# Feed-forward tokens normalised in halves, and the down projection's right factors made in the up phase

## The chip, the cores and the metric

The kernel runs on one core of a Trainium2 chip. The core has five engines that work side by side: TensorE (PE in the profile; its weight loads are PEld), VectorE (DVE), ScalarE (ACT), GpSimd (POOL) and SyncE (SP), which here only issues DMAs. Each engine takes its instructions strictly in the order in which the program was scheduled, and they wait for one another with semaphores. The metric is the device time of one execution in microseconds; lower is better.

## What is computed

One inference step of a two-layer decoder over 1024 prompt tokens, 16 learned tokens in front of them, and 8 x 8 sample tokens: 1104 token columns in layer 0 and 1088 in layer 1. The width is 1024 (`KD` = 8 blocks of 128 rows), the feed-forward width `D_FF` is 2816 (22 blocks of 128).

```python
def _trunk(h, ...):
    for layer in range(DEPTH):                        # 2
        if layer < N_A_LAYERS:                        # layer 0: Mamba-2
            mix, c, s = _mamba2_mixer(_rmsnorm(h, ssm_norm_g), ...)
        else:                                         # layer 1: window attention
            kv_in = _rmsnorm(h, kv_norm_g)            # shared K and V
            hn = _rmsnorm(h, attn_norm_g)
            mix = _sliding_sink_attention(hn @ w_q, k_all, v_all, ...) @ w_o
        h = h + mix
        hn = _rmsnorm(h, ffn_norm_g[layer])
        h = h + (jax.nn.silu(hn @ ffn_w_gate[layer]) * (hn @ ffn_w_up[layer])) @ ffn_w_down[layer]
    y = _rmsnorm(h, final_norm_g)
```

## The kernel before

**Arithmetic.** The data are float32. Every factor of a product is split into a high part H (a cast, on ACT) and a low part L (source minus H, a subtraction), and one product is three matmuls: H·H, H·L, L·H (`mm`, L1290 to L1293). The feed-forward products use a Strassen-Winograd scheme with seven products instead of eight (`PRODUCTS`): the left factors are the weight blocks A11 to A22 and four sums S1 to S4 of them, the right factors are the activation blocks B11 to B22 and the differences T1, T2, T3 and N4. Each product belongs to one of three PSUM lanes; the results are gathered from the lanes.

**Up phase** (`up`). The normalised tokens are cut into two row halves and two column halves, `h` = 552 columns each (544 in layer 1), so B11 and B21 belong to one half of the tokens, B12 and B22 to the other. A unit j is one block of 128 gate columns and one of 128 up columns; there are 22. A unit is seven products of 24 matmuls, 3696 matmuls per layer. `factor` (L1115 to L1123) makes one weight factor: ACT casts H (L1121), POOL subtracts L (L1122), and the sums S1 to S4 are made by DVE (L1113). After each product, `after_up` gathers lanes and applies the gate on DVE and ACT (L1327 to L1345) and sends the finished activations to DRAM (`act`).

**In front of the up phase** stands `normalise`. It starts when every residual column is done: sums of squares in `tot` (POOL, L1017), `row_scale` (L1028 to L1034 and the reciprocal root), `col_scale` (L1048 diagonals, a matmul L1049, a copy L1050), then for all 1104 columns the scaling (L1311), the differences (L1186) and the splits of seven right factors (ACT L1319, L by DVE or POOL L1320). The first steps of `up` are products 1 and 2 of two units, and wait for these splits.

**Down phase** (`down`). Five chunks of two Strassen units (1680 matmuls, tile `dacc`), then the last two row blocks as plain products (144 wide matmuls in layer 0, the same work by parts in layer 1; tile `wacc`, L69 to L71). The activations come back from DRAM (`ar`); DVE makes their differences (`bt`, L1186), ACT and DVE split them (`bo`, L1383 and L1384), POOL makes the weight sums and their low parts. The results are added to the residual tiles `hN` (DVE L1434; the sums X, Y, Z of the last chunk by POOL, L1437). In layer 0 the shared key and value product (`rps`) follows; at the end of layer 1 the final norm follows (transposes L1524, `Y` L1527, scaling L1542 and L1544).

**Order.** A tile scheduler turns this program into one list for each engine. SP's list holds all loads and stores, in one order.

## Time and profile before

| what | us |
|---|---|
| median of 3 runs | 3146.96 |
| lowest and highest run | 3145.66 and 3148.99 |
| the profiled execution's own time | 3141.77 |
| its span | 3140.0 |
| granted TensorE clock, mean | 0.958 |

The profile is one execution. Its span, from the first to the last instruction, is shorter than the execution's own time by 1.8 us. Busy shares of an engine over the span mix stages with different limits, so the stages are read apart: Mamba to about 1058, the first up phase to 1584, the first down phase to 1866, projections and attention to 2213, the output projection w_o to 2317, the second up phase to 2842, the second down phase with the final norm to 3140.

### The profile page before, as it was taken

How to read it: one execution, taken by the hardware profiler on the slowest of the kernel's cores; microseconds unless marked ns; L12 is line 12 of the kernel's file. 1: busy time of each engine (PE TensorE's matmuls, PEld its weight loads, DVE VectorE, ACT ScalarE, POOL GpSimd, SP SyncE). 2: the span in 40 equal slices, each digit the busy share in tenths (PEclk: the TensorE clock that was granted, in tenths of full speed). 3: DMA queues.
4: the chain of work that ended last, by engine and by line, in shares of the span. 5: the costliest groups of instructions: out<-in, count | busy, mean ns of one | idle time of the engine just before them, and what ended most of it. 6: DMA issues, size and time to landing. Idle time of an engine off the chain costs nothing.

```text
span 3140.0 us, 50718 instructions
## 1 busy us (share of the span) xinstructions
PE 2879.9 (92%) x19756; PEld 2607.1 (83%) x19756; DVE 2007.2 (64%) x3205; ACT 1132.2 (36%) x2296; POOL 1641.7 (52%) x1476
## 2 busy tenths in 40 slices
PE   7888989997999589999989989999967999998997
PEld 7777988875777489999989977766757999998997
DVE  6789676578685655545489970255246545548996
ACT  3444443344433332222233342356323222223332
POOL 2677565368564354444477763322225444447775
PEclk9999999998999789999999999999988999999999
DMA  4433423243332132222252120111013222225211
GB/s 117 130 119 103 143 85 108 90 136 114 98 111 77 58 118 77 74 78 77 82 179 86 41 69 21 43 35 31 14 57 110 73 79 76 83 73 186 83 43 65
DMA packets 298731, 270.17 MB, mean 86 GB/s; under 512 B 18604, under 2 KB 257644, under 8 KB 297950
## 3 DMA queue, kind: packets, MB, share of 16 engines
q1 hardware_dynamic: 298490, 266.92, 27.3%
q8 instruction: 156, 2.56, 0.3%
q14 instruction: 85, 0.69, 0.1%
HBM read 216.48 MB, written 50.40 MB: 85 GB/s over the span
## 4 chain that ended last, share of the span: by engine, by line
PE 65%; DVE 13%; POOL 4%; issue 3%; ACT 1%; DMA 0%; SPq 0%; POOLq 0%; ACTq 0%; DVEq 0%
PE wacc L1293 10%; PE wacc L1291 10%; PE wacc L1292 10%; PE acc L69 3%; PE acc L70 3%; PE acc L71 3%; PE dacc L1291 3%; PE dacc L1293 3%; PE dacc L1292 3%; DVE bt L1186 2%; DVE bo L1384 2%; PE rps L71 1%; PE rps L69 1%; PE rps L70 1%; PE ps L1734 1%
## 5 line engine op out<-in xcount | busy, mean ns | idle before, releaser
L1122 POOL TENSOR_TENSOR wo<-sum,wo 128x512 fp32r<-128x512 f32 x256 | 354.8, 1387 | 356.5 <-PE wacc L1293 247.2
L1122 POOL TENSOR_TENSOR wo<-ws,wo 128x512 fp32r<-128x512 f32 x216 | 300.4, 1394 | 331.0 <-PE wacc L1293 189.3
L1291 PE MATMUL dacc<-bo,wo 128*128 128x276 f32 (+1 forms) x1120 | 332.7, 300 | 29.3 <-DVE hN L1434 9.0
L1292 PE MATMUL dacc<-bo,wo 128*128 128x276 f32 (+1 forms) x1120 | 327.5, 293 | 6.6 <-DVE bo L1384 6.6
L1293 PE MATMUL dacc<-bo,wo 128*128 128x276 f32 (+1 forms) x1120 | 323.8, 293 | 6.3 <-POOL wo L1122 6.2
L69 PE MATMUL acc<-uH,wH 128*128 128x296 f32 (+1 forms) x960 | 329.0, 343 | 0.2
L71 PE MATMUL acc<-uH,wL 128*128 128x296 f32 (+1 forms) x960 | 326.2, 340 | 2.8 <-DVE wL L132 2.3
L70 PE MATMUL acc<-uL,wH 128*128 128x296 f32 (+1 forms) x960 | 326.2, 340 | 0.0
L1121 ACT CAST wo<-ws 128x512 fp32r<-128x512 f32 x216 | 133.6, 620 | 349.4 <-PE wacc L1293 192.5
L1291 PEld LDWEIGHTS dacc<-bo,wo 128*128 128x128 f32 x1120 | 214.4, 193 | 42.1 <-DVE hN L1434 14.0
L1121 ACT CAST wo<-sum 128x512 fp32r<-128x512 f32 x256 | 158.4, 619 | 235.0 <-PE wacc L1293 225.2
L1292 PEld LDWEIGHTS dacc<-bo,wo 128*128 128x128 f32 x1120 | 215.7, 193 | 7.5 <-DVE bo L1384 7.5
L1293 PEld LDWEIGHTS dacc<-bo,wo 128*128 128x128 f32 x1120 | 213.4, 192 | 7.3 <-POOL wo L1122 7.3
L132 POOL TENSOR_TENSOR wL<-ws,wH 128x512 fp32r<-128x512 f32 x112 | 158.9, 1439 | 113.1 <-ACT wH L126 104.2
L71 PEld LDWEIGHTS acc<-uH,wL 128*128 128x128 f32 x960 | 184.0, 192 | 21.6 <-issue 4.0
L69 PEld LDWEIGHTS acc<-uH,wH 128*128 128x128 f32 x960 | 184.9, 193 | 19.5 <-issue 4.1
L70 PEld LDWEIGHTS acc<-uL,wH 128*128 128x128 f32 x960 | 184.4, 192 | 18.7 <-issue 4.7
L551 DVE SCALAR_TENSOR_TENSOR cc<-raw,convw,cc 128x528 f32<-128x528 f32 (+1 forms) x216 | 176.7, 845 | 32.1 <-POOL cc L549 30.7
L126 ACT CAST wH<-ws 128x1024 fp32r<-128x1024 f32 x112 | 117.2, 1046 | 149.6 <-PE acc L70 104.4
L1291 PE MATMUL wacc<-B11H,wo 128*128 128x276 f32 (+1 forms) x352 | 106.7, 303 | 45.7 <-ACT B11H L1319 29.9
L69 PE MATMUL acc<-yH,wH 128*128 128x296 f32 (+1 forms) x384 | 133.1, 347 | 9.3 <-DVE hA L796 4.2
L1292 PE MATMUL wacc<-B11L,wo 128*128 128x276 f32 (+1 forms) x352 | 106.9, 304 | 26.6 <-DVE B11L L1320 26.6
(464 smaller groups left out, 9189.0 us busy)
## 6 DMA issues: line engine op xcount, KB each, us to landing
ws<-ssm_w_in SPq DMA_DIRECT2D x80, 512.0 KB
ws<-ffn_w_gate SPq DMA_DIRECT2D x44, 512.0 KB
ws<-ffn_w_up SPq DMA_DIRECT2D x44, 512.0 KB
ws<-ffn_w_down SPq DMA_DIRECT2D x44, 512.0 KB
E<-acsd SPq DMA_DIRECT2D x32, 512.0 KB
ws<-ssm_w_out SPq DMA_DIRECT2D x32, 512.0 KB
act<-temps SPq DMA_DIRECT2D x44, 276.0 KB
ar<-act SPq DMA_DIRECT2D x22, 552.0 KB
```

The costliest lines, as they stand in the source:

```text
L69: nc.tensor.matmul(out, wH, xH, start=start, stop=False)
L70: nc.tensor.matmul(out, wH, xL, start=False, stop=False)
L71: nc.tensor.matmul(out, wL, xH, start=False, stop=stop)
L126: self.nc.scalar.copy(H, w)
L132: eng.tensor_tensor(L[:, c], w[:, c], H[:, c].bitcast(F32), ALU.subtract)
L551: nc.vector.scalar_tensor_tensor(o, r(k), w(k), o, ALU.mult, ALU.add)
L1121: nc.scalar.copy(H, src)
L1122: nc.gpsimd.tensor_tensor(L, src, H.bitcast(F32), ALU.subtract)
L1186: nc.vector.tensor_tensor(t, a, b, ALU.subtract)
L1291: nc.tensor.matmul(out, wH, xH, start=start, stop=False, skip_group_check=True)
L1292: nc.tensor.matmul(out, wH, xL, start=False, stop=False, skip_group_check=True)
L1293: nc.tensor.matmul(out, wL, xH, start=False, stop=stop, skip_group_check=True)
```

## The change

The feed-forward object is split into `open`, `early`, `late`, `up` and `down`.

- **Halves.** `save` writes each residual half to DRAM. `early` normalises the half of the tokens that is ready, in place, and makes B11 and B21; it is stepped through between the last output tiles of the mixer (layer 0) or of w_o (layer 1). `late` does the other half, at the start of `up`.
- **First steps product by product.** The first three units (`FIRST` = 3) run interleaved in the order of `UP_FIRST`: three times product 1, three times product 2 (these need B11 and B21 alone), then 6, 7, 4, 5, 3. The right sums T1, T2, N4, T3 are made and split between these steps.
- **Weight sums** S2, S3, S4 are made in place, in the raw weight tiles; the low parts are subtracted by DVE. GpSimd keeps them for the first six steps and for products 7, 4 and 5 of the first three units.
- **Right factors of the down projection** are made during the up phase by queued tasks, one per step: a difference where needed, a split into a staging buffer (three of them), and a DMA to DRAM (`facts`, 77 of 565 KB in layer 0). `down` reads them back as ready `bo` tiles (six buffers) and splits nothing.
- **Down phase:** four chunks of two units and one of three, all seven products (1848 matmuls); no plain remainder. All adds are DVE's. The final norm, or the operands of the key and value product, are made tile by tile inside the last chunk.
- **w_o** runs in two token halves, 768 matmuls of 272 columns instead of 576 over the same columns; its weights are loaded and split twice.

```diff
+UP_FIRST = (1, 2, 6, 7, 4, 5, 3)
+DOWN_FIRST = (1, 6, 7, 4, 2, 5, 3)
...
-    def factor(self, name, engine):
+    def factor(self, name, low=None):
         nc = self.units.nc
-        src = self.source(name, engine)
+        src = self.source(name, nc.vector)
         H, L = (self.units.pool.tile([128, 512], F32R, name="wo", tag="wo", bufs=NOP)[:] for _ in range(2))
         nc.scalar.copy(H, src)
-        nc.gpsimd.tensor_tensor(L, src, H.bitcast(F32), ALU.subtract)
+        (low or nc.vector).tensor_tensor(L, src, H.bitcast(F32), ALU.subtract)
...
+        F.save(0)
+        early = F.early(self.psS)
+        for _ in self.out(G, hf, True):
+            for _ in range(6):
+                next(early, END)
+            yield
...
+    def late(self):
+        nc, K, s = self.nc, self.K, self.s
+        c0 = 592 if self.layer == 0 else self.h + s
+        blocks = [(c0 + 128 * i, 128) for i in range(4)]
+        if self.layer:
+            blocks = [(self.h, s)] + blocks
+        r = row_scale(K, blocks, self.wp, self.psS.tile([128, 512], F32, name="ps", tag="s"))
+        col_scale(K, blocks, r, self.psS)
+        if self.layer:
+            self.few(K.h[1][:, :, 8:40], [K.h[1][:, :, 0:32]], self.h)
+        h1 = K.h[1] if self.layer == 0 else K.h[1][:, :, 40:552]
+        for k in range(KD // 2):
+            for f in (k, k + 4):
+                self.scaled(h1[:, f], h1[:, f], f, c0)
...
+    def up_steps(self):
+        self.steps = [(j, p) for p in UP_FIRST for j in range(FIRST)] + [(j, p) for j in range(FIRST, self.nj) for p in UP_ORDER]
...
+            low = self.nc.gpsimd if self.at < 2 * FIRST or (self.at < 7 * FIRST and p in (7, 4, 5)) else self.nc.vector
...
+            if i == FIRST:
+                for k in range(KD // 2):
+                    self.right_sum("T1", k)
+                    self.right_sum("T2", k)
+                    self.right_split("T2", k)
...
+    def task(self, u, nm, at, terms=None):
+        def run():
+            nc = self.nc
+            if terms:
+                nc.vector.tensor_tensor(at, *terms, ALU.subtract)
+            st = self.stage[self.turn % 3]
+            self.turn += 1
+            split_copy(nc, st[:, 0], st[:, 1], at)
+            nc.sync.dma_start(self.facts[u][nm][:], st.bitcast(F32))
+        self.tasks.append(run)
...
+                for u in self.chunks[c]:
+                    t = dp.tile([128, 2, h], F32R, name="bo", tag="bo", bufs=NBO)
+                    nc.sync.dma_start(t[:].bitcast(F32), self.facts[u][PRODUCTS[p][2]][:])
...
-                        t = dp.tile([128, 2, h], F32R, name="bo", tag="bo", bufs=6)
-                        nc.scalar.copy(t[:, 0], src)
-                        nc.vector.tensor_tensor(t[:, 1], src, t[:, 0].bitcast(F32), ALU.subtract)
...
+            if p in own:
+                for h in ((h21, h12, h22), (h12,), (h22,))[own[p]]:
+                    add(h, into)
+            if p in (2, 4, 5, 3):
+                final.tile(p in (5, 3), mi + 4 * (p in (4, 5)))
```

The first place is DVE's list at the start of the first up phase. Before, from the first scaling of the tokens on (`ws` holds the scaled tokens, `tot` the scale of each column, `hA` and `big` the two residual halves):

```order
L1311 SCALAR_TENSOR_TENSOR ws<-hA,gains,tot 128x40 x8
L1311 SCALAR_TENSOR_TENSOR ws<-hA,gains,tot 128x512 x3
L1311 SCALAR_TENSOR_TENSOR ws<-big,gains,tot 128x512 x3
L1311 SCALAR_TENSOR_TENSOR ws<-hA,gains,tot 128x512
L1311 SCALAR_TENSOR_TENSOR ws<-big,gains,tot 128x512
L1320 TENSOR_TENSOR B11L<-ws,B11H 128x552
L1320 TENSOR_TENSOR B21L<-ws,B21H 128x552
```

The first product's right factor stood directly behind the scaling. In the changed kernel B11L and B21L are made ahead of this place, between the last adds of the mixer's output; behind the reciprocal root of `late` come:

```order
L1199 SCALAR_TENSOR_TENSOR big<-big,gains,tot 128x512 x8
L1274 TENSOR_TENSOR hA<-big,hA 128x552
L1380 SCALAR_TENSOR_TENSOR g_10201<-tf,wacc 128x552
L1274 TENSOR_TENSOR hA<-big,hA 128x552 x3
L1274 TENSOR_TENSOR sum<-big,hA 128x552
L1274 TENSOR_TENSOR big<-big 128x552
L78 TENSOR_TENSOR T1L<-hA,T1H 128x552
```

The scaling is of one half (`big`), 8 instructions; behind it stand the four T1 sums, the T2 sums (`sum`) and T3 sums (`big<-big`). The second place is some 25 rows further down the same list, where the third group of steps, product 6, gets its weight factor S2:

```order
L78 TENSOR_TENSOR N4L<-hA,N4H 128x552
L1050 TENSOR_TENSOR sum<-ws 128x512 x2
L78 TENSOR_TENSOR N4L<-hA,N4H 128x552 x2
L1050 TENSOR_TENSOR sum<-ws 128x512
L78 TENSOR_TENSOR N4L<-hA,N4H 128x552
L1053 TENSOR_TENSOR ws<-ws 128x512 x3
L1057 TENSOR_TENSOR ws<-sum,ws 128x512 x3
L1060 TENSOR_TENSOR ws<-ws 128x512 x2
L1069 TENSOR_TENSOR wo<-ws,wo 128x512
```

L1050, L1053, L1057 and L1060 are S1, S3, S2 and S4 of the first three units, L1069 the first low part of S2. All of it stands behind the T and N splits. The third place is DVE's list where the down phase of layer 0 starts. Before, differences and splits of activations (`ar`, `bt`) stand in front of the first add:

```order
L1186 TENSOR_TENSOR bt<-ar,bt 128x552
L1186 TENSOR_TENSOR bt<-ar 128x552 x2
L1384 TENSOR_TENSOR bo<-ar,bo 128x552
L1384 TENSOR_TENSOR bo<-bt,bo 128x552 x3
L1186 TENSOR_TENSOR bt<-ar,bt 128x552 x2
L1384 TENSOR_TENSOR bo<-bt,bo 128x552
L1434 TENSOR_TENSOR hN_15193<-hN_15193,dacc 128x552
```

Now weight factors stand there (L1069) with one late task (`big<-hA,big`), and no `bo` is written by DVE:

```order
L78 TENSOR_TENSOR big<-hA,big 128x552
L1069 TENSOR_TENSOR wo<-ws,wo 128x512 x2
L1060 TENSOR_TENSOR ws<-ws 128x512 x2
L1069 TENSOR_TENSOR wo<-sum,wo 128x512 x2
L1508 TENSOR_TENSOR hN_15545<-hN_15545,dacc 128x552 x3
L1069 TENSOR_TENSOR wo<-ws,wo 128x512
L1508 TENSOR_TENSOR hN_15545<-hN_15545,dacc 128x552
```

The `bo` tiles are filled from SP's list instead, by loads of `facts`.

More of the change, by code (lines that the diff above doesn't have):

```diff
@@ new lines, in down, with after_down @@
+        final.close()
+    def after_down(self, XYZ, c, p, mi, ps, final):
+        nc, K = self.nc, self.K
+        add = lambda d, s: nc.vector.tensor_tensor(d, d, s, ALU.add)
+        last = c == len(self.chunks) - 1
+        own = {1: 0, 6: 1, 7: 2}
+        if p in own:
+            into = XYZ[own[p]][:, mi]
+        if p not in own or last:
+            h11, h12, h21, h22 = (K.h[e][:, mi + 4 * f, :] for f in range(2) for e in range(2))
+        if p not in own:
+            into = {2: h11, 4: h21, 5: h22, 3: h12}[p]
@@ new lines, in tile @@
+    def tile(self, e, m):
+        nc, K, h = self.nc, self.K, self.h
+        e = int(e)
+        src = K.h[e][:, m, :]
+        dst = K.tot[:, h * e : h * e + h]
+        first = self.seen[e] == 0
+        t = dst if first else self.pool.tile([128, h], F32, name="sqf", tag="sqf", bufs=2)[:]
+        nc.scalar.activation(t, src, AF.Square)
+        if not first:
+            nc.vector.tensor_tensor(dst, dst, t, ALU.add)
+        self.seen[e] += 1
+        if m % 2:
+            self.work.append(lambda: self.turn(e, (m - 1, m), range(4)))
+        if m % 4 == 3:
+            self.ready = getattr(self, "ready", [0, 0])
+            self.ready[e] += 1
+            if self.ready[e] == 2:
+                self.work.append(lambda: self.turn(e, range(KD), (4,)))
+                self.work.append(lambda: self.part(e))
+        if self.now[1] in (5, 3) and self.work:
+            self.work.pop(0)()
@@ new lines, in tile @@
+    def tile(self, e, m):
+        nc, K = self.nc, self.K
+        e, f = int(e), m // 4
+        if (e, f) == (1, 1) and m == 4:
+            L = [self.wp.tile([128, 512], F32R, name="sum", tag="sum", bufs=NSUM)[:] for _ in range(4)]
+            self.parts[1, 1] = self.new("uH1"), L
+        if (e, f) == (1, 0):
+            t = self.wp.tile([128, 2, 552], F32R, name="bo", tag="bo", bufs=NBO)
+            H, L = t[:, 0, :512], t[:, 1, :512]
+        else:
+            H, L = self.parts[e, f]
+            H = H[:, m % 4]
+            L = L[m % 4] if type(L) is list else L[:, m % 4]
+        self.U[e][m] = H, L
+        src = K.h[e][:, m, 40:552]
+        dst = K.tot[:, 512 * e : 512 * e + 512]
+        first = self.seen[e] == 0
+        t = dst if first else self.sq
+        nc.scalar.activation(t, src, AF.Square)
+        if not first:
+            nc.vector.tensor_tensor(dst, dst, t, ALU.add)
+        split_copy(nc, H, L, src)
+        self.seen[e] += 1
+        if self.seen[e] == KD:
+            self.small(e)
@@ L1901, in load_wo @@
                 return load
-            for m in range(KD):
-                F.units.plain(load_wo(m))
+            for m in range(2 * KD):
+                F.units.plain(load_wo(m % KD))
             F.units.queue += ups
```

948 lines of the change are left out of this document (516 added, 432 removed).

## The prediction

> **What bounds the kernel now.** I read the page's head first, then the windows by stage, then what the waits in the bad windows end on.
>
> ```profile
> span 3140.0 us, 50718 instructions
> PE 2879.9 (92%) x19756; PEld 2607.1 (83%) x19756; DVE 2007.2 (64%) x3205; ACT 1132.2 (36%) x2296; POOL 1641.7 (52%) x1476
> ```
>
> TensorE is busy for 92% of the span, so a gain comes only from its idle stretches: the change adds matmuls, it does not remove any. The windows show where PE is idle; the columns are the stretch, its length, busy time and instructions of PE, PEld, DVE, ACT and POOL, the granted clock, the DMA share and the rate.
>
> ```profile
> 1040.00:1058.00 18.00, 18.00 (x84) 14.61 (x82) 6.41 (x9) 6.36 (x10) 11.05 (x9) 1.00 0.04 9
> 1058.00:1070.00 12.00, 5.76 (x32) 5.29 (x31) 6.82 (x33) 2.65 (x6) 1.76 (x2) 0.72 0.47 175
> 1070.00:1090.00 20.00, 4.23 (x13) 3.06 (x13) 18.75 (x29) 8.57 (x14) 8.18 (x3) 0.55 0.00 0
> 1090.00:1112.00 22.00, 3.64 (x12) 2.68 (x12) 20.76 (x31) 9.90 (x17) 8.50 (x5) 0.50 0.47 157
> 1112.00:1118.00 6.00, 3.16 (x12) 2.82 (x13) 6.00 (x4) 2.42 (x5) 6.00 (x4) 0.50 0.56 151
> 1118.00:1584.00 466.00, 465.68 (x3662) 465.46 (x3661) 227.81 (x281) 130.51 (x216) 207.27 (x157) 1.00 0.24 77
> 1590.00:1838.00 248.00, 231.06 (x1702) 223.93 (x1703) 228.53 (x244) 89.35 (x156) 190.40 (x125) 0.97 0.27 91
> 1838.00:1868.00 30.00, 23.80 (x126) 20.65 (x126) 29.25 (x43) 21.79 (x61) 14.17 (x6) 0.93 0.16 44
> ...
> 2213.00:2221.00 8.00, 5.07 (x14) 3.05 (x14) 7.73 (x16) 8.00 (x21) 0.00 (x0) 0.65 0.00 0
> 2234.00:2317.00 83.00, 82.58 (x500) 75.23 (x498) 10.75 (x31) 16.88 (x39) 29.47 (x17) 1.00 0.03 8
> 2317.00:2334.00 17.00, 7.94 (x36) 7.53 (x36) 7.97 (x38) 3.41 (x8) 2.47 (x1) 0.70 0.78 263
> 2334.00:2356.00 22.00, 4.98 (x16) 3.83 (x17) 20.77 (x34) 9.63 (x15) 8.07 (x3) 0.52 0.00 0
> 2356.00:2380.00 24.00, 4.18 (x14) 2.89 (x12) 22.77 (x32) 10.20 (x17) 12.97 (x7) 0.50 0.57 180
> 2380.00:2842.00 462.00, 461.85 (x3666) 461.85 (x3667) 227.23 (x281) 131.06 (x218) 208.93 (x157) 0.99 0.24 77
> 2846.00:3085.00 239.00, 221.12 (x1653) 213.91 (x1654) 224.83 (x237) 87.72 (x153) 186.52 (x123) 0.97 0.28 96
> 3131.00:3140.00 9.00, 0.35 (x2) 0.26 (x2) 2.42 (x12) 1.15 (x1) 0.00 (x0) 0.50 0.56 221
> ```
>
> Two things stand out. The steady up phase (1118 to 1584, 2380 to 2842) is full: PE at 466 of 466 us. But each transition into it, 1058 to 1118 and 2317 to 2380, is nearly empty on PE while DVE is busy for 19 to 23 of 20 to 24 us. The down phases (1590 to 1838, 2846 to 3085) lose 17 and 18 us, with DVE at 92% to 94%. The starts of the stages, by tile:
>
> ```profile
> L71 PE MATMUL acc<-yH,wL x384: 292/301/797, 284.9 to 1057.1; 128*128 128x296 f32 x128, 128*128 128x512 f32 x64
> L1291 PE MATMUL dacc<-bo,wo x1120: 284/290/599, 1588.3 to 3088.3; 128*128 128x276 f32 x94, 128*128 128x272 f32 x93
> L69 PE MATMUL rps<-rwH,fuH x200: 387/393/628, 1866.2 to 2020.1; 128*128 128x512 f32 x96, 128*80 128x512 f32 x4
> ```
>
> The price of an up matmul is 465.68 / 3662 = 0.1272 us in layer 0 and 461.85 / 3666 = 0.1260 in layer 1. Its 3696 matmuls are 470 and 466 us of work. From 1057.5 to 1584 are 526.5 us, from 2317 to 2842.4 are 525.4: the **transitions lose 56 and 60 us**. Who ends the waits of the first one:
>
> ```profile
> PE wacc L1291 <- ACT B11H L1319: 14.9, 3, 7.6
> PE wacc L1292 <- DVE B11L L1320: 13.1, 4, 4.9
> PE wacc L1291 <- ACT wo L1121: 10.8, 2, 7.9
> ```
>
> Right factors and weight factors, that is the DVE and ACT queue of the normalisation.
>
> **The transition of layer 0.** B11 and B21 are now made beside the last output tiles, so six steps (products 1 and 2 of three units, 144 matmuls, 144 x 0.1272 = 18.3 us) can run at once, at the clock of a busy PE. What is late next is the seventh step, product 6: it needs T2 and the weight sum S2, both from DVE, in order. DVE's price per instruction when GpSimd rests is in the timeline (start, length):
>
> ```profile
> 1061.57 0.16 DVE L1033 TENSOR_SCALAR rv<-ps 80x1 f32<-80x1 f32 x1 [3.34 <-PE ps L1028]
> ...
> 1066.68 1.46 DVE L1311 SCALAR_TENSOR_TENSOR ws<-hA,gains,tot 128x40 f32<-128x40 f32 x8 [1.18 <-ACT tot L1050]
> ...
> 1073.79 0.73 DVE L1320 TENSOR_TENSOR B11L<-ws,B11H 128x552 fp32r<-128x552 f32 x1
> 1074.43 0.73 DVE L1320 TENSOR_TENSOR B21L<-ws,B21H 128x552 fp32r<-128x552 f32 x1
> ```
>
> and its price next to GpSimd in the groups of the window 1058 to 1112 (busy time, mean ns):
>
> ```profile
> L1320 DVE TENSOR_TENSOR T2L<-sum,T2H 128x552 fp32r<-128x552 f32 x4 | 4.1, 1020 | 0.0
> ```
>
> Instructions of 0.73 us start every 0.64 us. Counted from the end of the mixer's last matmul: the row sums stand behind 41 up matmuls in PE's list (5.2 us), so their result comes at about 6.5 us rather than 4.1 (1061.57 less 1057.5). From there to the first scaling were 5.1 us (1066.68 less 1061.57), so 11.6; eight scalings at 0.66 end at about 17. Down to the first low part of S2 are then 47 instructions in DVE's list, 47 x 0.645 = 30.3 us, which gives 47. GpSimd makes low parts in this stretch and slows some of them: 1 to 4 us more, I take 1. So PE waits from 18.3 to about 48, **30 us**, and then restarts at half the clock, about 2 us more, as the 0.50 of the row 1112:1118 shows over 6 us. Loss 32 against 56: **gain 24**. Bounds: if T2 and S2 came as early as their data allow (16 instructions of DVE less), the gain is 34; if all 47 took 1.02 us, the mean of T2L, 47 x 0.375 = 18 us more and the gain some 8.
>
> TensorE: Matmul & The Clock Gate, § What's actually happening, in the Trainium skill, says that an idle window of about 3.4 us halves the array's clock and that about 3.4 us of work bring it back. That speaks against one long gap; by it the restart costs 1.7 us, by the row up to 3, and the trace agrees that the clock is 0.50 after the gaps.
>
> **The transition of layer 1** has the same order behind w_o's second half, with one row block more: loss 33 against 60, **gain 27**, bounds 10 and 37.
>
> **Steady up phase.** Here the change moves work to DVE, and the durations decide:
>
> ```profile
> L1345 DVE SCALAR_TENSOR_TENSOR temps<-temps 128x552 f32<-128x552 f32 x21 | 33.1, 1574 | 0.7
> L1344 DVE SCALAR_TENSOR_TENSOR temps<-temps 128x552 f32<-128x552 f32 x21 | 15.3, 728 | 1.6 <-ACT temps L1343 1.6
> L1336 DVE TENSOR_TENSOR temps<-temps,wacc 128x552 f32<-128x552 f32 x22 | 16.1, 730 | 15.8 <-PE wacc L1293 15.8
> L1122 POOL TENSOR_TENSOR wo<-sum,wo 128x512 fp32r<-128x512 f32 x88 | 115.3, 1311 | 159.4 <-PE wacc L1293 125.3 <-issue 34.1
> ```
>
> L1344 and L1345 are the same operation on the same tiles; the one falls beside a GpSimd subtraction and takes 1574 ns, the other does not and takes 728. L1336 reads PSUM and keeps 730. In the changed list a unit has 25.5 DVE instructions: 7 low parts, 4 weight sums, 9 of `after_up`, 3.5 task splits and 2 task differences. With GpSimd idle that is 25.5 x 0.73 = 18.6 us of a unit's 168 x 0.1272 = 21.4. PE stays the bound, with 2.8 us to spare: **0**. The 7/2 stores of 565 KB add 2.0 MB per unit, or 93 GB/s, to the 77 in the row. If the cover is gone, all 38 later units pay: above 21.4 / 25.5 = 0.84 us per instruction PE waits for DVE.
>
> The Trainium skill (SBUF — State Buffer, § Who interferes with whom) has GpSimd and a DVE instruction with two SBUF inputs take one port pair in turn, the loser blocked for a whole instruction. By that rule the slow values go with GpSimd and the sum stays 18.6; if 1574 belonged to two-input work as such, the 19.5 instructions without PSUM would need 30.7 us, a unit 35, and a layer 260 us more. The trace agrees with the rule: 728 against 1574, and 730 from PSUM.
>
> **Down phase of layer 0.**
>
> ```profile
> L1384 DVE TENSOR_TENSOR bo<-bt,bo 128x552 fp32r<-128x552 f32 x40 | 51.9, 1334 | 0.0
> L1434 DVE TENSOR_TENSOR hN<-hN,dacc 128x552 f32<-128x552 f32 x80 | 55.2, 721 | 13.3 <-PE dacc L1293 11.2 <-POOL hN L1437 2.0
> ```
>
> From 1584 to 1866.2 are 282.2 us. After: 1848 x 0.1272 = 235.1. The splits (L1384) go, the weight factors of the first chunk are made before the up phase ends, and the loads of `bo` are 1.13 MB per two-unit step of 12.2 us. What transfers do at their best in this kernel is the rate of the window 2842 to 2850, where activations are read back:
>
> ```profile
> DMA packets 802, 2.86 MB, mean 358 GB/s; under 512 B 80, under 2 KB 80, under 8 KB 802
> ```
>
> 1.13 MB is 3.2 us at that rate. I put 1 us at the start, 4 for scattered waits. The last chunk is new: 504 matmuls, 64 us, in which DVE has about 96 instructions, 96 x 0.70 = 67 us, unevenly: product 1's step carries 16 adds and the weight sums. PE has four PSUM buffers to run ahead and then waits: 11 us (5 to 18). Sum 251, **gain 31**, bounds 15 and 42.
>
> **w_o.** From 2213 to 2317 are 104 us; the work is the same number of columns in 768 narrower matmuls. A second split of the weights (16 more pairs on ACT and DVE) hides beside PE; DVE is at 10.75 of 83 us. The wait at the start (2213:2221, PE 5.07 of 8) shrinks, since half of the tokens suffice: **gain 3**, bounds -5 and 5.
>
> **Second down phase and end.** From 2842.4 to 3140 are 297.6. After: 1848 x 0.126 = 232.8, 11 us of transposes, 6 at the start and scattered, 12 in the last chunk (DVE has more there: final-norm products and squares), and an end of 16 against 9 in the row 3131:3140, since half of the tokens leave at the end instead of a quarter: 278, **gain 20**, bounds 0 and 32.
>
> **Mamba's tail.** `early` puts 8 scalings, 8 splits and a row scale, 15 to 20 us of DVE work, beside the last output tiles, on a DVE with 6.41 of 18 us used (1040 to 1058), but next to GpSimd's squares. Nothing else of the mixer changes: **-3**, bounds -8 and 0.
>
> **Sum:** 24 + 27 + 0 + 31 + 3 + 20 - 3 = 102. The profiled span 3140.0 becomes 3038, its execution 3141.77 becomes 3040. The median of the runs, 3146.96, is 5.2 above that execution, so the forecast is **3045**. All low bounds together give 20 less (8 + 10 + 15 - 5 + 0 - 8), 3127; all high ones 150, 2997.
>
> **Rivals.**
> - *The queue takes the place of the waits.* DVE beside GpSimd's low parts in the transitions, and a fully DVE-bound last chunk: gains of 8 and 10 in the transitions, 24 and 12 in the down phases, 51 in all: 3096. For it: DVE was the busy engine in exactly these windows. Against: GpSimd has at most 15 low parts there, 15 x 1.311 = 20 us of 48. Chance 0.2.
> - *DVE becomes the bound of the up phase*, the slower side. Place: the 38 units behind the first three in the two layers; point: 0.84 us per instruction. At a mean of 1.0, each unit takes 25.5 instead of 21.4, 38 x 4.1 = 156 us, less the gain of 102: slower by 54, 3201. For it: 87% load and staging buffers that wait for their stores in one SP list. Against: 728 and 730 at 77 GB/s of traffic. Chance 0.05.
> - *Reads of the factors are late*: 43.5 MB of `bo` plus 11.5 MB of weights in 235 us want 234 GB/s, against 91 and 96 before. At 200 GB/s the two phases take 40 us more each: 3125. Chance 0.05.
> - *The waits vanish earlier* than DVE's list lets me believe, and last chunks stall half as long: 3005. Chance 0.1.
>
> **How the numbers follow.** The forecast (3025 to 3075) has 0.6; the rivals 0.2, 0.05, 0.05 and 0.1. The range 2998 to 3112 takes in the forecast, the first and the last rival. Of the late reads' 0.05, 0.02 may end at no change. Faster by over 0.2% (6 us, about what a measurement of this kernel can tell from no change): 0.93; within it 0.02; slower 0.05.
>
> **What would show it.** Right: in the transitions one PE gap of 25 to 35 us behind six full steps, ended by a low part of a weight or T2; the DVE subtractions of the up phase at 0.73 us; the up windows full; dacc from start to `rps` in about 250 us. Wrong: mean DVE durations near 1 us with GpSimd idle, waits of PE for weight factors all through the up phase, or waits for DMA at `dacc`.

## The result and the profile after

| | before | after |
|---|---|---|
| median, us | 3146.31 (3145.48 to 3148.99, 4 runs) | 3030.12 (3028.85 to 3031.24, 4 runs) |
| ratio | 1 | 0.9629, 95% interval 0.9613 to 0.9646 |
| span of the profiled execution, us | 3140.0 | 3028.6 |
| granted TensorE clock, mean | 0.958 | 0.968 |

The kernel became 116 us faster; the forecast was 3045 in a range of 2998 to 3112. The profiled execution of before lay 4.5 us below its median and that of after at its median, so the spans differ by 111. The head of the page of after:

```profile
span 3028.6 us, 51155 instructions
PE 2836.6 (94%) x19952; PEld 2597.2 (86%) x19952; DVE 2159.5 (71%) x3810; ACT 1159.2 (38%) x2298; POOL 771.2 (25%) x881
```

GpSimd has lost half of its time, DVE has gained 152 us, and PE's share rose by two points. Where the time went is read from the starts of the stages, by tile (the kernel of after; count, shortest, median and longest duration in ns, first and last start):

```profile
L73 PE MATMUL acc<-yH,wL x384: 292/301/797, 285.3 to 1072.5; 128*128 128x296 f32 x128, 128*128 128x512 f32 x64
L1366 PE MATMUL dacc<-bo,wo x1232: 283/289/569, 1580.1 to 3008.0; 128*128 128x276 f32 x88, 128*128 128x272 f32 x88
L1366 PE MATMUL dacc<-bo,wo x616: 283/288/566, 2763.3 to 3008.0; 128*128 128x272 f32 x154
L71 PE MATMUL rps<-rwH,u x96: 388/397/504, 1822.3 to 1951.9; 128*128 128x512 f32 x96
L71 PE MATMUL wacc<-OH,wo x256: 284/287/457, 2162.2 to 2262.8; 128*128 128x272 f32 x128
```

The second `dacc` row is the answer for the window from 2600 on, layer 1. In the profile of before the second down phase began at 2846.7 and w_o at 2213.3.

| stage | before, us | after, us | change | forecast |
|---|---|---|---|---|
| to the end of the mixer's output | 1057.5 | 1072.9 | +15.4 | +3 |
| from there to the first `dacc` (transition and up phase) | 530.8 | 507.2 | -23.6 | -24 |
| to the first `rps` (down phase, layer 0) | 277.9 | 242.2 | -35.7 | -31 |
| to the start of w_o (projections, attention) | 347.1 | 339.9 | -7.2 | 0 |
| to the second `dacc` (w_o, transition, up phase) | 633.4 | 601.1 | -32.3 | -30 |
| to the end (down phase, final norm) | 293.3 | 265.3 | -28.0 | -20 |
| sum | 3140.0 | 3028.6 | -111.4 | -102 |

The windows of after, in the columns of the prediction: the output of the mixer, the six covered steps, the gap, its end, the steady up phases, the first four chunks and the last chunk of both down phases, and the end.

```profile
1045.00:1073.00 28.00, 18.77 (x77) 14.95 (x76) 25.13 (x24) 14.53 (x24) 20.65 (x13) 0.82 0.38 112
1073.00:1091.00 18.00, 18.00 (x145) 18.00 (x145) 8.21 (x24) 3.71 (x6) 2.58 (x2) 1.00 0.08 30
1091.00:1119.00 28.00, 2.24 (x17) 2.01 (x16) 28.00 (x45) 12.44 (x20) 0.00 (x0) 0.62 0.00 0
1119.00:1150.00 31.00, 30.67 (x220) 30.13 (x221) 15.06 (x23) 7.71 (x14) 13.88 (x9) 0.91 0.25 73
1150.00:1570.00 420.00, 419.81 (x3293) 419.59 (x3292) 326.96 (x506) 164.25 (x271) 0.00 (x0) 1.00 0.42 148
2330.00:2750.00 420.00, 420.00 (x3355) 420.00 (x3354) 328.42 (x512) 166.90 (x274) 1.70 (x2) 1.00 0.43 148
1580.00:1758.00 178.00, 175.02 (x1349) 174.34 (x1350) 139.08 (x216) 51.48 (x84) 0.00 (x0) 0.98 0.79 287
1758.00:1822.00 64.00, 63.48 (x501) 63.25 (x499) 59.92 (x98) 27.12 (x47) 0.14 (x2) 1.00 0.44 150
2938.00:3010.00 72.00, 72.00 (x584) 71.73 (x584) 64.97 (x111) 21.57 (x34) 0.10 (x1) 1.00 0.39 133
3010.00:3029.00 19.00, 4.08 (x30) 3.64 (x27) 10.50 (x26) 3.40 (x4) 0.00 (x0) 0.65 0.61 235
```

The transition is now what the prediction drew: a stretch of full PE at a clock of 1.00, then 28 us in which DVE is busy for all 28 and PE for 2. The up phase is as full as before with DVE at 78%. PE is busy for 63.48 of 64 and for 72.00 of 72 us of the last chunks. The window 1045:1073 is the surprise: PE 18.77 of 28 us where 18.00 of 18 stood before. What PE waits for, by length, over the mixer's tail with the first transition, then over the first down phase (in the program's words; sum, times, longest):

```profile
PE wacc L1366 <- ACT wo L1068: 25.8, 1, 25.8
PE acc L71 <- DVE big L798: 9.2, 1, 9.2
...
PE dacc L1366 <- DMA bo<-f_B: 6.2, 2, 4.5
```

The timeline of DVE, ACT and GpSimd in after shows both places (start, length, instruction, idle time ahead of it). First the gap:

```profile
1078.98 0.16 DVE L1002 TENSOR_SCALAR rv<-ps 128x4 f32<-128x4 f32 x1 [5.39 <-PE ps L996]
...
1085.93 5.39 DVE L1199 SCALAR_TENSOR_TENSOR big<-big,gains,tot 128x512 f32<-128x512 f32 x8 [4.01 <-ACT tot L1018]
1091.24 0.73 DVE L1274 TENSOR_TENSOR hA<-big,hA 128x552 f32<-128x552 f32 x1
...
1109.89 0.73 DVE L78 TENSOR_TENSOR T2L<-sum,T2H 128x552 fp32r<-128x552 f32 x1
...
1117.35 1.90 DVE L1057 TENSOR_TENSOR ws<-sum,ws 128x512 f32<-128x512 f32 x3
...
1118.09 3.38 ACT L1068 CAST wo<-ws 128x512 fp32r<-128x512 f32 x6 [7.42 <-DVE ws L1057]
...
1120.36 0.70 DVE L1069 TENSOR_TENSOR wo<-ws,wo 128x512 fp32r<-128x512 f32 x1
```

DVE runs without a break from 1085.9; from 1091.24 to the end of the first low part of S2 at 1121.1 are 29.8 us for 47 instructions. PE starts again at 1118.8 with the cast of S2, though all of T2 is ready at 1110.6. DVE was idle for 5.4 and 4.0 us just ahead. Then the mixer's tail:

```profile
1049.41 13.64 DVE L1199 SCALAR_TENSOR_TENSOR hA<-hA,gains,tot 128x592 f32<-128x592 f32 x8
...
1062.98 0.72 DVE L78 TENSOR_TENSOR B11L<-hA,B11H 128x552 fp32r<-128x552 f32 x1
1063.62 0.67 DVE L798 TENSOR_TENSOR big<-big,acc 128x512 f32<-128x512 f32 x1
...
1053.58 3.58 POOL L1069 TENSOR_TENSOR wo<-ws,wo 128x512 fp32r<-128x512 f32 x2
1057.12 3.54 POOL L134 TENSOR_TENSOR wL<-ws,wH 128x512 fp32r<-128x512 f32 x2
1060.62 1.79 POOL L1069 TENSOR_TENSOR wo<-ws,wo 128x512 fp32r<-128x512 f32 x1
```

Eight early scalings (592 columns) stand in one block ahead of an output add (L798) for which PE waits, and each takes 1.77 us while GpSimd works without a break beside them; the eight scalings at 1085.93 (512 columns), with GpSimd idle, take 5.39 us in all, 0.67 each. Behind the wait the output matmuls start every 0.43 us until 1070 where they started every 0.23 before it, and the granted clock of the window is 0.82.

### The profile page after: what moved, and what is told of

Same layout as the page of the kernel before. It is cut to its first block, busy times and chain, and to the rows that moved or that the text cites. A ratio compares the mean times of both kernels' runs of the same rounds, so it can differ in the third digit from the quotient of the medians.

```text
span 3028.6 us, 51155 instructions
## 1 busy us (share of the span) xinstructions
PE 2836.6 (94%) x19952; PEld 2597.2 (86%) x19952; DVE 2159.5 (71%) x3810; ACT 1159.2 (38%) x2298; POOL 771.2 (25%) x881
## 4 chain that ended last, share of the span: by engine, by line
PE 71%; DVE 7%; POOL 3%; DMA 2%; issue 2%; ACT 0%; SPq 0%; ACTq 0%; POOLq 0%; DVEq 0%
PE wacc L1368 10%; PE wacc L1366 10%; PE wacc L1367 10%; PE dacc L1366 5%; PE dacc L1367 5%; PE dacc L1368 5%; PE acc L71 3%; PE acc L72 3%; PE acc L73 3%; PE rps L71 2%; PE rps L73 2%; PE rps L72 2%; PE ps L1891 1%; PE po L1939 1%; PE po L1940 1%
## 5 line engine op out<-in xcount | busy, mean ns | idle before, releaser
L1068 ACT CAST wo<-ws 128x512 fp32r<-128x512 f32 x428 | 263.9, 620 | 586.9 <-PE wacc L1367 222.2
L1366 PE MATMUL dacc<-bo,wo 128*128 128x276 f32 (+1 forms) x1232 | 360.0, 292 | 15.2 <-DMA bo<-f_B 10.6
L1367 PE MATMUL dacc<-bo,wo 128*128 128x276 f32 (+1 forms) x1232 | 357.8, 290 | 0.0
L1368 PE MATMUL dacc<-bo,wo 128*128 128x276 f32 (+1 forms) x1232 | 357.7, 290 | 0.0
L1069 DVE TENSOR_TENSOR wo<-ws,wo 128x512 fp32r<-128x512 f32 x404 | 279.0, 694 | 50.7 <-ACT wo L1068 43.0
L1366 PEld LDWEIGHTS dacc<-bo,wo 128*128 128x128 f32 x1232 | 234.3, 190 | 16.5 <-issue 15.2
L1367 PEld LDWEIGHTS dacc<-bo,wo 128*128 128x128 f32 x1232 | 234.3, 190 | 0.0
L1368 PEld LDWEIGHTS dacc<-bo,wo 128*128 128x128 f32 x1232 | 234.1, 190 | 0.0
L72 PEld LDWEIGHTS acc<-uL,wH 128*128 128x128 f32 x960 | 184.6, 192 | 18.4 <-issue 4.5
L134 POOL TENSOR_TENSOR wL<-ws,wH 128x512 fp32r<-128x512 f32 x112 | 158.9, 1440 | 116.1 <-ACT wH L128 109.5
L128 ACT CAST wH<-ws 128x1024 fp32r<-128x1024 f32 x112 | 117.1, 1045 | 142.1 <-PE acc L72 92.8
L1366 PE MATMUL wacc<-T2H,wo 128*128 128x276 f32 (+1 forms) x352 | 104.9, 298 | 51.5 <-ACT wo L1068 51.5
L1508 DVE TENSOR_TENSOR hN<-hN,dacc 128x544 f32<-128x544 f32 (+1 forms) x164 | 116.4, 721 | 27.0 <-PE dacc L1368 21.2
L72 PE MATMUL acc<-yL,wH 128*128 128x296 f32 (+1 forms) x384 | 132.1, 345 | 0.0
```

The lines of the kernel that those rows point to most:

```text
L72: nc.tensor.matmul(out, wH, xL, start=False, stop=False)
L128: self.nc.scalar.copy(H, w)
L134: eng.tensor_tensor(L[:, c], w[:, c], H[:, c].bitcast(F32), ALU.subtract)
L1068: nc.scalar.copy(H, src)
L1069: (low or nc.vector).tensor_tensor(L, src, H.bitcast(F32), ALU.subtract)
L1366: nc.tensor.matmul(out, wH, xH, start=start, stop=False, skip_group_check=True)
```

## The experiments

Times are compared by the ratio to the kernel before on the same chip; the changed kernel's is 0.9629. 0.001 is 3.1 us.

### e1 to e4: the mixer's tail, GpSimd's share, and the end of the gap

e1, spaced scalings (`paced`):

```diff
-            for _ in range(6):
+            for _ in range(2):
                 next(early, END)
...
-                self.scaled(h0[:, f, :592], h0[:, f, :592], f, 0)
+                gd = self.units.sums.tile([128, 1], F32, name="gd", tag="gd", bufs=KD)
+                nc.vector.tensor_scalar(gd[:], K.h[1][:, (f + 1) // 2, 0:1], 0.0, self.gain[:, f : f + 1], ALU.mult, ALU.add)
+                nc.vector.scalar_tensor_tensor(h0[:, f, :592], h0[:, f, :592], gd[:], K.tot[:, 0:592], ALU.mult, ALU.mult)
```

> In the changed kernel the eight early scalings of layer 0 stand in one block ahead of the fourth output add, take 13.64 us beside GpSimd, and TensorE waits 9.2 us for that add. Here each scaling takes its gain through a small copy that also reads a finished output tile (added as zero), so two scalings at most stand between two adds; nothing else changes. Theory A (the order of DVE's list costs the Mamba tail): the wait of 9.2 us and the slow clock behind it, some 2 us, go, the output ends near 1061 instead of 1072.9, and the time falls by 8 to 12 us, to about 3020. Theory B (DVE beside GpSimd has too little room in this stretch whatever the order): the same work only waits elsewhere, the output ends within 3 us of 1072.9 or the sixth step behind it is late by as much, and the time stays within 3 us of 3030.

e2, no low part on GpSimd, and e3, all low parts of the up phases on GpSimd, change one line:

```diff
-            low = self.nc.gpsimd if self.at < 2 * FIRST or (self.at < 7 * FIRST and p in (7, 4, 5)) else self.nc.vector
+            low = self.nc.vector
```

```diff
-            low = self.nc.gpsimd if self.at < 2 * FIRST or (self.at < 7 * FIRST and p in (7, 4, 5)) else self.nc.vector
+            low = self.nc.gpsimd
```

> All low parts of weight factors on DVE, also those of the first six steps and of products 7, 4 and 5 of the first three units, which the changed kernel left on GpSimd. Theory A (order): the block of eight scalings stays, so most of the 9.2 us wait stays; the time within 3 us of 3030. Theory B (the scalings are slow because GpSimd's low parts hold the shared access to SBUF): the block falls from 13.64 us to 6 to 9 us, the wait from 9.2 to 2 to 4, and the time falls by 5 to 7 us in layer 0. In layer 1, whose w_o leaves DVE idle, both expect nothing from this. The nine low parts behind the gap go from GpSimd to DVE, 9 x 0.64 = 6 us of DVE beside 27 us of TensorE: no cost expected.

> Low parts of the up phase back on GpSimd in all 22 units of both layers, the rest as in the changed kernel. By the prediction's price DVE falls from 25.5 to 18.5 instructions per unit, but 12.5 of them read SBUF twice and meet seven GpSimd subtractions of 1.3 us: mean durations of the task splits and gate products rise from 0.73 to 1.1 to 1.5 us. If DVE and GpSimd exclude each other fully, DVE's 18.5 x 0.73 = 13.5 plus GpSimd's 9.4 are 22.9 us of 21.4 per unit and TensorE waits 1.5 us per unit, 38 units, 57 us: about 3087. If the six instructions that read PSUM run beside GpSimd, 22.9 less 4.4 fit into 21.4, TensorE stays full and the time stays within 6 us of 3030. Rival: the durations belong to the instructions, not to GpSimd; then they stay at 0.73 here.

e4, early S2:

```diff
+        for j in range(2):
+            self.made[j].src["place"] = ft.tile([128, 512], F32, name=f"s1{j}")[:]
+            self.made[j].source("S2", nc.vector)
         self.late()
...
-                s["S1"] = self.units.sum()[:, :512]
+                s["S1"] = s.pop("place") if "place" in s else self.units.sum()[:, :512]
```

> The sums S1, S3 and S2 of the first two units get a place of their own for S1 and stand ahead of the second half's normalisation, where DVE is idle for 5.4 and 4.0 us; nothing else changes. In the changed kernel product 6 waits 25.8 us for S2 in both transitions, although T2L of the first row block is ready at 1104.2, 14.6 us ahead of it, and the last at 1110.6. Theory (the queue of DVE with S2 at its end sets the gap): the gap ends with T2 instead, the first unit's product 6 is paced by the four T2L and ends at about 1111.5 instead of 1121.9, so 8 to 11 us per transition, 16 to 22 in all: 3008 to 3014. Rival (T2 and the T sums set the gap, the sums of the weights come for nothing): the gap shrinks by less than 3 us each and the time stays above 3024.

| run | median, us | ratio, 95% interval |
|---|---|---|
| e1 spaced scalings | 3025.82 | 0.9620 (0.9605 to 0.9635) |
| e2 no low parts on GpSimd | 3027.36 | 0.9622 (0.9606 to 0.9639) |
| e3 low parts on GpSimd | 3040.13 | 0.9670 (0.9650 to 0.9691) |
| e4 early S2 | 3017.59 | 0.9591 (0.9569 to 0.9612) |

**e1 and e2 only move the wait.** Both times lie within the noise of the changed kernel, and absolute times inside one profile don't compare well here: the mixer's own length differs from run to run (its last `dg` matmul starts between 1027.7 and 1046.8; the latest is the profile of e2, which is the longest of its four runs). Lengths of stages compare. The output stage, from that matmul to the last output matmul, takes 26.9 us before (1030.2 to 1057.1), 39.9 after (1032.6 to 1072.5), 36.2 in e1 and 36.1 in e2. But from that last output matmul to the first `dacc` (transition and up phase), after takes 507.6 us, e1 511.6 and e2 510.5: the 3.7 and 3.8 us saved in the output stage are paid back behind it, all of it in e1 and 2.9 us in e2. That is theory B of e1, while of e2 the time is as theory A had it. In e1 the scalings are spaced but still take 1573 ns; in e2 they take 1265 ns in a block, so GpSimd's low parts account for a good part of the 1772; its squares and the mixer's own low parts (L986, L134) still stand in this stretch. PE waits less at one place and again at the next (e1, over the tail; the second row is the first up matmul that waits for an output add):

```profile
PE acc L71 <- DVE big L798: 4.4, 2, 3.0
PE wacc L1368 <- DVE big L798: 3.1, 1, 3.1
```

**e3** shows what GpSimd's part in the up phase is worth. The groups of the window 1150 to 1570 in e3, and the same line in after:

```profile
L1387 DVE SCALAR_TENSOR_TENSOR hA<-hA,big 128x552 f32<-128x552 f32 x18 | 31.4, 1743 | 0.6
...
L1386 DVE TENSOR_TENSOR hA<-big,wacc 128x552 f32<-128x552 f32 x18 | 13.1, 730 | 35.0 <-PE wacc L1368 35.0
```

```profile
L1387 DVE SCALAR_TENSOR_TENSOR hA<-hA,big 128x552 f32<-128x552 f32 x18 | 13.1, 727 | 0.0
```

The gated multiply, whose two inputs lie in SBUF, takes 1743 ns beside GpSimd and 727 without it; the add that reads PSUM (L1386) keeps 730. Yet the phase hardly suffers. The steady windows of e3:

```profile
1150.00:1570.00 420.00, 415.86 (x3257) 414.77 (x3257) 332.68 (x369) 158.21 (x268) 188.24 (x136) 1.00 0.42 146
2330.00:2750.00 420.00, 415.33 (x3295) 414.09 (x3295) 332.19 (x368) 155.84 (x266) 193.48 (x137) 1.00 0.43 144
```

DVE needs 332.7 us for 369 instructions, 0.90 each, where after needs 327.0 for 506, 0.65 each; both stay below 420, so PE gives up only 4 to 5 us in either window. By time e3 is 0.0041, or 13 us, above the changed kernel, between the two theories; the two stretches of transition and up phase are 6.8 and 8.1 us longer, of which the first low part of S2, now made by GpSimd, holds PE up for 2.1 us each time where DVE's held it for 0.3. In the changed order of work, then, leaving the low parts to DVE is worth some 13 us of the 116.

**e4** shows what the gap consists of. Its waits of PE (sum, times, longest), first transition:

```profile
PE wacc L1370 <- DVE T2L L78: 5.8, 1, 5.8
PE wacc L1369 <- ACT wo L1068: 5.4, 1, 5.4
PE wacc L1369 <- ACT T2H L77: 3.4, 1, 3.4
PE wacc L1369 <- DVE g L1383: 1.5, 1, 1.5
```

The one wait of 25.8 us has become four that sum to 16.1; in layer 1 the same 25.8 became 17.5. That is 9.7 + 8.3 = 18 us off the two gaps, as the theory of DVE's order had it. The raw weights were there early: e4 makes S2 of two units by 1074, ahead of the second half's scaling. S2 stood at the end of DVE's list because S1 takes one of four buffers (`sum`) that the T2 sums hold until their splits are done, and e4 gives S1 a place of its own. Most of what remains ends with T2. The two stretches of transition and up phase became 8.1 and 6.2 us shorter. In time it is 0.0038, 12 us; the median, 3017.6, falls short of the theory's 3008 to 3014, the four runs lie further apart than those of the other kernels (3009 to 3023), and the profile is the shortest of them.

### e5 and e6: T2 first, and the two repairs of the tail together

The lists are ordered by the scheduler, so e5 (`t2first`) changes the order through data. It is e4 with dependences added: the sums of N4 and T3 are multiplied by a one that is computed from the last T2 low part and from the third unit's S2, and the casts of T1 and N4 by a one computed from the last T3 low part.

```diff
-        self.nc.vector.tensor_tensor(d, a, b, ALU.subtract)
+        if nm in ("T3", "N4"):
+            self.nc.vector.scalar_tensor_tensor(d, a, self.gate(nm), b, ALU.mult, ALU.subtract)
+        else:
+            self.nc.vector.tensor_tensor(d, a, b, ALU.subtract)
+
+    def after(self, nm, src):
+        self.nc.vector.tensor_scalar(self.gate(nm), src, 0.0, 1.0, ALU.mult, ALU.add)
...
+                self.after("N4", self.right["T2"][1][:, 3, 0:1].bitcast(F32))
+                self.after("T3", self.made[2].source("S2", nc.vector)[:, 0:1])
```

> As the run with early S2, and DVE's list in the transition is put into the order of need: the sums of N4 and T3 and the splits of T1 and N4 are tied, through a factor of one, to the last T2L, to S2 of the third unit and to the last T3L. So the last T2L stands 15 instructions behind the scaling instead of 30, then S2 of the third unit, then T3. Nothing is left out; a few tiny instructions are added. Theory (the gap is DVE's queue, instruction by instruction): the last T2L comes at 15 x 0.645 = 9.7 us behind the end of the scaling instead of 19.4, product 6 ends that much earlier, and later products wait 0 to 4 us: 6 to 10 us per transition less than with early S2 alone, 12 to 20 in all, about 3000 where the run with early S2 has 3017.6. Rival (another engine is next in line, ACT's casts or PSUM): the waits only change their names and the time stays within 5 us of 3017.6.

e6 (`paced_nogp`) joins the edits of e1 and e2.

> The spaced scalings together with all low parts on DVE: both suspects of the Mamba tail at once. Each alone left 8.4 to 9 us of waits there. Theory A+B (order and GpSimd's grip on the shared access each cost the other's gain: spaced scalings of 1573 ns still come too late, fast scalings in a block still stand ahead of the adds): waits of the tail fall to 0 to 4 us and the time to 3018 to 3023. Rival C (DVE has too much to do in 27 us of output matmuls whatever its speed: 8 scalings, 8 splits, 8 adds, one wL and six low parts are 31 instructions and 23 us, and GpSimd's squares and wL remain): waits stay at 6 to 9 us and the time at 3025 to 3028.

| run | median, us | ratio, 95% interval |
|---|---|---|
| e5 T2 first | 3009.62 | 0.9558 (0.9544 to 0.9572) |
| e6 spaced and no low parts on GpSimd | 3027.13 | 0.9611 (0.9597 to 0.9626) |

PE's waits in e5's first transition:

```profile
PE wacc L1391 <- DVE wo L1069: 7.1, 1, 7.1
PE wacc L1389 <- ACT T2H L77: 3.5, 1, 3.5
PE wacc L1390 <- DVE T2L L78: 1.5, 1, 1.5
```

T2 now costs 5.0 us where e4 lost 9.2 to it, and the waits of the gaps are 12.1 and 14.2 us: 4.0 and 3.3 less than in e4. The two stretches of transition and up phase are 3.6 and 0.4 us shorter than e4's. The ratio is 0.0033 lower, 10 us, but the two intervals overlap at their ends. All of this is short of the theory's 12 to 20 us, because a new wait came up: the low part of the third unit's S2 (L1069) now stands behind the sums of T3. Order on DVE decides again, one place further down, and not alone: three of the four T3 sums take 1.79 us each beside GpSimd's low parts, where the first takes 0.79 without them.

In e6 the output stage takes 33.0 us (1038.0 to 1071.0), 6.9 less than in the changed kernel, where e1 alone saved 3.7 and e2 3.8. There the two repairs nearly add up; from the last output matmul to the first `dacc`, though, e6 takes 510.6 us, 3.0 more than after, so 3.9 us are left. The scalings take 1239 ns. The waits for output adds are 4.7 us, above the 0 to 4 of the theory and below the 6 to 9 of the rival; the median lies in the rival's range. The ratio moved by 0.0018, 6 us, and the intervals of e6 and the changed kernel still overlap, so the profile's stages carry this and not the time.

### e7 and e10: fewer units product by product

`FIRST = 3` becomes 2 in e7 and 1 in e10. PE's covered work ahead of the gap is then 12.2 and 6.1 us instead of 18.3.

> Two units instead of three run product by product; everything else as in the changed kernel. By the prediction's sum the cover ahead of product 6 is four steps (12.2 us) instead of six (18.3), and DVE's list up to S2 is shorter by about 5 instructions (S1, S3, S2 and S4 of one unit and one gate product, 3 us): the gap grows by 3 us per transition, 6 in all, and behind it the four steps of products 7 and 4 cover less of N4, T1 and B22, 0 to 4 us more: 3036 to 3040. Rival (the cover is not used, the gap is as long as DVE's queue): the time falls by the shorter queue, 3024. Two units also leave the first tasks earlier, no effect expected.

> One unit instead of three runs product by product at the start of both up phases; else as the changed kernel. With two units the gap ended by S2 was 30.6 instead of 25.8 us, 4.8 more per unit and transition, where the sum had 3. Theory (cover less 6.1 us, queue shorter by what a unit's sums and gate product take, 1.3 to 3 us): the gap is 34 to 36 us and the time 3042 to 3050, with the first wait on S2 still the long one. Rival (with one unit S1 finds a free buffer ahead of the T2 sums, since only one of four is wanted, and the gap ends with T2 instead): the gap is 25 to 30 us, the time 3030 to 3038.

| run | median, us | ratio, 95% interval |
|---|---|---|
| e7 two units | 3038.37 | 0.9644 (0.9628 to 0.9661) |
| e10 one unit | 3035.07 | 0.9640 (0.9624 to 0.9656) |

```profile
PE wacc L1366 <- ACT wo L1068: 30.6, 1, 30.6
...
PE wacc L1366 <- ACT T2H L77: 10.3, 1, 10.3
PE wacc L1366 <- DVE big L1377: 4.8, 1, 4.8
```

The first row is e7: the gap grew by 4.8 us (30.5 against 25.8 in layer 1, too), 6.1 us less cover against fewer DVE instructions ahead of S2. The other two are e10: the long wait for S2 is gone in layer 0, as the rival had it, since with one unit S1 takes its buffer ahead of the T2 sums; PE's longest wait there ends with T2. In layer 1 two waits of 12.1 us stand in its place, for T2 and for a low part that GpSimd makes. Neither time can be told from the changed kernel's. The stretches of transition and up phase can: in e7 they are 6.0 and 4.2 us longer than after's, in e10 1.6 shorter and 6.1 longer. So a shorter head start costs something, and with one unit a shorter list ahead of S2 pays it back in layer 0 alone. (Fewer early steps also leave GpSimd fewer low parts beside the mixer's tail: its scalings take 1391 ns in e7 and 1646 in e10.)

### e8: each read of the factors twice

```diff
                     nc.sync.dma_start(t[:].bitcast(F32), self.facts[u][PRODUCTS[p][2]][:])
+                    nc.sync.dma_start(t[:].bitcast(F32), self.facts[u][PRODUCTS[p][2]][:])
```

> Each right factor of the down phases is read from DRAM twice into the same buffer, the second load behind the first; nothing else changes. It measures what the prediction's rival of late reads had at stake. Reads of factors grow from 43.5 to 87 MB per phase beside 11.5 MB of weights: 98.5 MB in 235 us want 419 GB/s, where the changed kernel moved 287 GB/s at a DMA share of 0.79 in the first four chunks. Theory (transfers are near their limit already): at 358 GB/s the phases take 275 us each, 35 us more, 70 in all, and more where a DMA waits for the one ahead: 3100 to 3150. Rival (there is room, loads run three steps ahead): within 10 us of 3030.

Measured: 3097.15, ratio 0.9835 (0.9815 to 0.9854), 67 us above the changed kernel, 3 us under the theory's lower end and far from the rival. Windows of the two down phases, and PE's waits in the first:

```profile
1590.00:1768.00 178.00, 157.75 (x1172) 155.79 (x1173) 113.98 (x175) 42.77 (x69) 0.00 (x0) 0.94 1.01 402
2790.00:2960.00 170.00, 143.61 (x1076) 141.55 (x1076) 107.71 (x169) 39.15 (x65) 0.00 (x0) 0.92 0.97 384
...
PE dacc L1366 <- DMA bo<-f_B: 16.9, 2, 13.2
PE dacc L1366 <- DMA bo<-f_N: 9.7, 1, 9.7
```

The queues run at a share of 1.01 and 402 GB/s, and PE waits for `bo`. After moves 287 GB/s in this stretch. So its reads are hidden, but with a margin of 402 / 287 = 1.4 by rate, or 1.01 / 0.79 = 1.3 by share, under a factor of two.

### e9: everything together

e9 joins e1, e4 and the gates of e5 (T3's sums now tied to the low part of the third unit's S2), and moves the low parts of the first six steps from GpSimd to DVE.

```diff
-            low = self.nc.gpsimd if self.at < 2 * FIRST or (self.at < 7 * FIRST and p in (7, 4, 5)) else self.nc.vector
+            low = self.nc.gpsimd if 2 * FIRST <= self.at < 7 * FIRST and p in (7, 4, 5) else self.nc.vector
...
+                    if k == 0:
+                        self.after("T3", self.left[8][1][:, 0:1].bitcast(F32))
```

> All of it together: spaced scalings, low parts of the first six steps on DVE, early S2 of two units, DVE's list in the order of need, and now the sums of T3 tied to the low part of the third unit's S2 (it stood behind them in the run before and cost 7.1 us in each transition). Nothing is left out. Theory (the waits are DVE's queue and add up): the output stage of the mixer takes about 33 us as with both tail edits instead of 39.9, the gaps fall from 25.8 to 6 to 8 us in each transition; from the run with the order of need, 3009.6, 7 us and 2 x 4 us go: 2992 to 3000. Rival (each time a wait is taken away the next in line takes its place): 3004 to 3010.

Measured: 3011.78, ratio 0.9562 (0.9547 to 0.9576); it can't be told from e5, and it lies above the theory's range and just above the rival's. PE's waits in the first transition, then GpSimd and DVE ahead of the longest of them:

```profile
PE wacc L1394 <- DVE big L1405: 8.0, 1, 8.0
PE wacc L1394 <- ACT T2H L77: 3.2, 1, 3.2
PE wacc L1395 <- DVE T2L L78: 1.3, 1, 1.3
...
1108.36 8.20 POOL L1069 TENSOR_TENSOR wo<-ws,wo 128x512 fp32r<-128x512 f32 x5 [32.29 <-ACT wo L1068]
...
1108.71 6.72 DVE L1278 SCALAR_TENSOR_TENSOR big<-big,one 128x552 f32<-128x552 f32 x4
```

The wait for the weight factor is gone and one of 8.0 us has taken its place, in both layers: the add that frees the PSUM lane of product 6 (L1405) now stands behind T3's splits. The order is one reason; the other is that GpSimd makes low parts there, and the four T3 sums take 6.72 us beside them, 1.7 each. No run joins this order with all low parts on DVE. The output stage takes 34.1 us (1034.5 to 1068.6), better than after's 39.9, but the two stretches behind it are 3.0 and 1.9 us longer than e5's. e5 and e9 both beat the changed kernel by 0.7%, about 20 us.

The stages that the edits touch, in us, counted from start to start of matmuls; the last column is by how much the sum of the three differs from the changed kernel's:

| run | output stage | last output matmul to `dacc`, layer 0 | last w_o matmul to `dacc`, layer 1 | against after |
|---|---|---|---|---|
| before | 26.9 | 531.2 | 530.4 | +40.8 |
| after | 39.9 | 507.6 | 500.2 | 0 |
| e1 | 36.2 | 511.6 | 500.4 | +0.5 |
| e2 | 36.1 | 510.5 | 500.2 | -0.9 |
| e3 | 38.5 | 514.4 | 508.3 | +13.5 |
| e4 | 40.0 | 499.5 | 494.0 | -14.2 |
| e5 | 39.8 | 495.9 | 493.6 | -18.4 |
| e6 | 33.0 | 510.6 | 500.7 | -3.4 |
| e7 | 37.0 | 513.6 | 504.4 | +7.4 |
| e9 | 34.1 | 498.9 | 495.5 | -19.2 |
| e10 | 39.8 | 506.0 | 506.3 | +4.4 |

In e1, e2 and e6, whose edits were expected to change nothing in layer 1, its stretch agrees with after's within 0.5 us, so differences of some us in this table mean something. The last column follows the ratios: 0.001 there is 3.1 us here.

## Why the prediction was right or wrong

The forecast, 3045, is 15 us above the measured 3030. The mechanism is the one forecast in the transitions and the up phases; one term failed outright, and two others were too cautious. That the total came so close is in part luck: the tail cost 12.4 us more than forecast, attention gave 7.2 that nobody forecast, and the down phases gave 12.7 more than their terms. Another 5 of the 15 us come from the 5.2 that the forecast added for the distance of a profiled execution from the median, which after does not have.

- **Transitions: right.** Six steps ran at full clock, from 1072.7 to 1093.0; these 20.3 us (forecast 18.3) hold the row scale's matmuls too. PE then waited 25.8 us (forecast 30). Counted from the last output matmul at 1072.9, the row sums came at +6.1 us (6.5), the first scaling at +13.0 (11.6), its end at +18.3 (17), then 47 DVE instructions in 29.8 us (30.3), and PE restarted at +45.9 (48). The matmuls behind the restart start every 0.23 us until 1124.7, where they take 0.127 at full clock, and lose about 3 us (forecast 2). The stages gained 23.6 us, and 32.3 with w_o (2.2 in w_o itself), against 24 and 30. e4 and e5 show the reason too: change what stands ahead of S2 and T2 on DVE, and the gap shrinks. The bound "as early as their data allow", 10 us better than the forecast, was about right: e5 took 13.7 and 11.6 us off the waits of the two gaps, and 11.7 and 6.6 off the stretches.
- **Steady up phase: right, 0.** PE is busy 419.8 and 420.0 of 420 us. The task splits' subtractions (L78) take 730 ns once GpSimd rests. The load came to 78% instead of 87%, because such instructions start every 0.645 us, which the prediction had used for the transition but not here. e3 shows that the slower form was not deadly either: putting GpSimd beside DVE costs 13 us, while the adds that read PSUM are not slowed. The condition of the DVE-bound rival, a mean above 0.84 us, did not come up: after's mean is 0.65. In e3 it is 0.90, but there GpSimd carries the low parts and DVE has 369 instructions instead of 506 in the window.
- **Down phase of layer 0: the sign and the cause right, a size off.** 35.7 us against 31. The step that was mis-sized is the stall in the last chunk, put at 11 us: 63.48 of 64 us are busy. Its price of 0.70 us per instruction was too high, as 98 instructions took 59.92 us, 0.61 each, so DVE keeps ahead. The start was worse than put: PE waits 4.5 us for the first `bo` rather than 1. The 358 GB/s that the sum took as the best rate of transfers was only the mean of the window chosen: in the next stretch of before, 2848 to 2856, it is 406. That these stages gain because the splits are gone is read from the traces; no run puts the splits back.
- **Second down phase and end: the same step.** 28.0 against 20. The last chunk was forecast to lose 12 us and is full (72.00 of 72); the end took 19 us instead of 16.
- **Mamba's tail: wrong, outside its bounds.** Forecast a loss of 3 us (0 to 8), measured a loss of 15.4. Of this 13.0 are the output stage itself, 26.9 to 39.9 us; the other 2.4 were there ahead of it, less than the mixer varies between runs. The step that failed is "15 to 20 us of DVE work on a DVE with 6.41 of 18 us used". It counted capacity and not order. Eight scalings stand as one block ahead of an add that frees PE's buffer; they meet GpSimd's own block of additions and subtractions and take 1.77 us each, 13.64 us in all. The trace accounts for nearly all of the 13.0: PE waits 9.2 us, loses 2.4 with matmuls that start every 0.43 instead of 0.23 us behind the wait, and spends 1.0 on the row scale's matmuls (L1017) in between. The prediction had the very row that prices this (1574 beside 728) and used it only for the up phase. e6 got 6.9 us of the 13.0 back by spacing the scalings and taking the low parts from GpSimd, but lost 3.0 again in the steps behind; what is left in its output stage is 2.6 us of the same wait, some 2 of slow matmuls and 1 for the row scale.
- **Attention** gained 7.2 us that were not forecast. Most of it lies where attention starts: of 40 us there (2022 to 2062) PE is busy for 33.66 at a clock of 0.74 before, and for 37.68 at 0.87 after (1978 to 2018). In the runs of e1 to e10, which leave attention as it is, the stage takes 335.9 to 341.3 us. Why it is shorter than before stays open.
- **Rivals.** The queue took the place of the waits in the gap alone, as drawn in the forecast, and not in the last chunks. Reads came late by 4.5 and 4.4 us at the two starts, and throughout only when doubled (e8). DVE never became the bound of the up phase. Of the rival that waits vanish earlier, the part on the last chunks came true and more: they hardly stall.
